# Splitting the recurrence's gate weights: four pieces on ScalarE and VectorE instead of two on GpSimd

## The chip, the cores and the metric

One NeuronCore of a Trainium2 chip runs the whole program. The metric is device time in microseconds (us) for one execution; lower is better. Five engines work side by side, each through its own queue in order: TensorE (PE: matmuls and transposes), VectorE (DVE), ScalarE (ACT), GpSimd (POOL) and SyncE (SP, which issues most DMAs). They wait for one another through semaphores.

## The reference, cut to what matters

A two-layer encoder on 256 tokens of width 1024. Each layer is a SwiGLU block, a mixing step whose two head groups run side by side (a gated linear recurrence, RG-LRU, and windowed attention), and another SwiGLU block:

```python
for l in range(DEPTH):                       # DEPTH = 2
    x = x + 0.5 * swiglu(rms_norm(x, ffn1_norm[l]), ffn1_w_gate[l], ffn1_w_up[l], ffn1_w_down[l])
    h = rms_norm(x, mix_norm[l])
    xr, gate, q, k, v = jnp.split(h @ w_in[l], SPLITS, axis=-1)
    y = concat([rms_norm(recurrent_group(xr, gate, ..., w_a, w_x, ...)), rms_norm(windowed_gqa(q, k, v, ...))])
    x = x + y @ w_out[l]
    x = x + 0.5 * swiglu(rms_norm(x, ffn2_norm[l]), ffn2_w_gate[l], ffn2_w_up[l], ffn2_w_down[l])
return rms_norm(x, final_norm)

# in recurrent_group, for each of two directions d: gates from small block-diagonal weights
r = sigmoid(einsum('bsnc,ncd->bsnd', xb, w_a[d]) + b_a[d])    # 8 blocks of 64 x 64
i = sigmoid(einsum('bsnc,ncd->bsnd', xb, w_x[d]) + b_x[d])
```

## The kernel before, in words

Inputs and outputs are float32. For TensorE every weight `w` is split into a rounded part `wh` (of type fp32r) and the rest, `wl = w - wh`, activations likewise, and a product is the sum of three: high by high, high by low, low by high. The splitting is a stream of its own. SP loads raw weights in pieces of 1 MB into three buffers (`raw`). From each, ACT makes `wh` (L297, 128x1024) and DVE makes `wl` (L298, 128x1024) into a ring of eight slots; a raw buffer is loaded again when both of its halves are split, and a slot is filled again when TensorE has used it.

Six stages follow one another: for each layer a SwiGLU stage (`ffn`), a mixing stage (`mix`) and a second `ffn`. The two `ffn` stages that open a layer are the places of this change; I call them the opening stages of layer 0 and of layer 1. In an `ffn`, the hidden units come in 22 blocks `m` of 128. The first two are done token-major in the head (`natural`, L544, for the first `ffn` `first_head`, L701), gated by ACT (tanh, L724) and DVE (L725, L726), and transposed on TensorE into one PSUM bank (`head_end`, L718), which ACT and DVE split into `hh` and `hl` (L732, L733). From m = 2 on, `gu` runs the gate and the up projection of a block (16 or so matmuls each, L563 to L566) into PSUM, `whole` adds the halves (`sg` and `su`: ACT L744, DVE L745), `gated` and `split_h` make `hh` and `hl` for the down projection, `dn` (L573 to L575). PSUM has two banks under the name `ps_g` and two under `ps_c`, which these projections and the transposes take in turn: a projection has to wait until ACT and DVE have emptied the bank that it gets.

The orders of PE, SP and POOL are as the program is written. Those of ACT and DVE are set by the scheduler that builds the program, by its own estimate of when an instruction becomes ready. Each queue is then worked off in that order.

The gate weights of the recurrence, `gw` (two kinds a, two directions d, four tiles of 128x128: 128x2048 in all), are loaded by POOL in each opening stage: at m == `GLOAD` (4), `load_gates` clears the tile (L355) and issues four DMAs for each a (L359, eight in all per stage). Since POOL has nothing else to do, it does so as soon as its queue comes there. At m == `GSPLIT` (8), `split_gates` lets POOL make `gh_t` (a rounding copy, L369, 128x1024 for each a) and `gl_t` (a subtraction with two SBUF operands, L370, 128x1024 for each a). They are used a stage later, by `lru_gate` in the mixing stage (L887 to L889).

Of the kernel before, what the change touches and what calls it, by code (L numbers as in the profile page):

```python
# [8 lines left out]
F32 = mybir.dt.float32  # L9
F32R = mybir.dt.float32r  # L10
AF = mybir.ActivationFunctionType
ALU = mybir.AluOpType
# [20 lines left out]
TAIL = 4  # L33
HB = 7
GLOAD = 4
GSPLIT = 8
X1 = False
EXTRA = {("kv", 0): "w", ("kv", 1): "i"}
if X1:
# [28 lines left out]
def encoder_kernel(  # L68
# [31 lines left out]
    pe, act, dve, pool = nc.tensor, nc.scalar, nc.vector, nc.gpsimd  # L100
# [250 lines left out]
    gw = []  # L351

    def load_gates(l):
        gw.append(mix_p.tile([128, 2, 2, NT, 128], F32, tag="i", name="gw"))
        pool.memset(gw[l], 0.0)  # L355
        for a, w in ((0, lru_w_a), (1, lru_w_x)):
            for d in range(2):
                for e in range(2):
                    pool.dma_start(  # L359
                        out=gw[l][64 * e:64 * e + 64, a, d, :, 64 * e:64 * e + 64],  # L360
                        in_=w[l, d].rearrange("(t e) c o -> e c t o", e=2)[e],
                    )

    gh_t = const.tile([128, 2, 2, NT, 128], F32R, name="gh_t")
    gl_t = const.tile([128, 2, 2, NT, 128], F32R, name="gl_t")

    def split_gates(l):
        for a in range(2):
            pool.tensor_copy(out=gh_t[:, a], in_=gw[l][:, a])  # L369
            pool.tensor_tensor(out=gl_t[:, a], in0=gw[l][:, a], in1=gh_t[:, a].bitcast(F32), op=ALU.subtract)  # L370

    def load_x(t):
        for hf in range(2):
# [54 lines left out]
    def setup_params():  # L428
        tmp = a_p.tile([128, 2, 512], F32, tag="a", name="tmp")
        rows_t = tmp[:N_ROWS, 0, :]  # L430
        srcs = [(R_CONVW, conv_w.rearrange("l j c -> (l j) c")), (R_CONVB, conv_b),
                (R_BA, lru_b_a.rearrange("l d c -> (l d) c")), (R_BX, lru_b_x.rearrange("l d c -> (l d) c")),
                (R_LAM, lru_lambda.rearrange("l d c -> (l d) c")), (R_GREC, lru_out_norm), (R_GATT, attn_out_norm)]
        for r, s in srcs:
            pool.dma_start(out=rows_t[r:r + s.shape[0], :], in_=s)
        pool.dma_start(out=sink_t, in_=attn_sink.partition_broadcast(128))
        rb = mix_p.tile([128, T], F32, tag="k", name="rb")[:33, :NH]
        oh = tmp[:33, 1, :]
        pool.memset(rb[32:33, :], -1e30)
        pool.dma_start(out=rb[0:32, :], in_=rel_bias)  # L440
        pool.dma_start(out=oh, in_=onehot)
        return tmp, rows_t, rb, oh
# [231 lines left out]
    def ffn(st, acc_done):  # L674
# [38 lines left out]
        def head_end():  # L713
            ps = bank("gc")
            for t in range(2):
                for m in range(2):
                    c = m * T + t * 128
                    pe.transpose(ps[:, c:c + 128], hn_t[t][:, m * 128:(m + 1) * 128], eye_t)  # L718
            for m in range(2):
                split_h(m, ps[:, m * T:(m + 1) * T])  # L720

        def gated(g, u):
            th = ep_p.tile([128, T], F32, tag="th", name="th")
            act.activation(out=th, in_=g, func=AF.Tanh, scale=0.5)  # L724
            dve.scalar_tensor_tensor(out=th, in0=th, scalar=1.0, in1=g, op0=ALU.add, op1=ALU.mult)  # L725
            late["gated"] = dve.tensor_tensor(out=th, in0=th, in1=u, op=ALU.mult)  # L726
            return th

        def split_h(m, src):
            hh = h_p.tile([128, T], F32R, tag="hh", name="hh")  # L730
            hl = h_p.tile([128, T], F32R, tag="hl", name="hl")
            act.activation(out=hh, in_=src, func=AF.Copy)  # L732
            dve.tensor_sub(out=hl, in0=src, in1=hh.bitcast(F32))  # L733
            hh_t[m] = (hh, hl)

        def gu(m, nm):
            ps = gu_ps[m, nm] = bank("gc")
            proj_pair(ps, W(st, nm, m))
            done((st, nm, m))

        def whole(m, nm):
            ps = gu_ps.pop((m, nm))
            s = sum_p.tile([128, T], F32, tag="s" + nm, name="s" + nm)
            act.activation(out=s, in_=ps[:, T:2 * T], func=AF.Copy)  # L744
            dve.tensor_tensor(out=s, in0=ps[:, 0:T], in1=s, op=ALU.add)  # L745
            return s

        def dn(m, t, hfs, fin):
            if t not in acc:
                acc[t] = [bank("ab"[t]) for _ in range(2)]  # L750
            hh, hl = hh_t[m]
            for hf in hfs:
                end = NM - TAIL if st == (DEPTH - 1, 2) and (t, hf) == (1, 1) else NM
                stream(acc[t], hh, hl, W(st, "d", m), t, (hf,), m == 0, m == end - 1)
            if fin:
                done((st, "d", m))
                del hh_t[m]
# [24 lines left out]
        def body():  # L782
            nd = 0
            for m in range(HEAD, NM):
                if m >= RAMP:
                    state["ahead"] = min(DAHEAD, state["ahead"] + 1)
                gu(m, "g")
                g = whole(m, "g")
                gu(m, "u")
                split_h(m, gated(g, whole(m, "u")))  # L790
                if m == HEAD:
                    head_end()
                if st == (0, 0):
                    if m == 4:
                        late_setup.append(setup_params())
                    if m == 9:
                        setup_params2(*late_setup.pop())
                if st[1] == 0 and m == GLOAD:
                    load_gates(st[0])
                if st[1] == 0 and m == GSPLIT:  # L800
                    split_gates(st[0])
                while nd <= m - LAG and nd < NM - TAIL and m > HEAD:
                    dn(nd, 0, (0, 1), False)
                    dn(nd, 1, (0, 1), True)
                    nd += 1
            while nd < NM - TAIL:
                dn(nd, 0, (0, 1), False)
                dn(nd, 1, (0, 1), True)
                nd += 1

        if st == (DEPTH - 1, 2):
            tail, evac = dn_cols, acc
        return head if st != (0, 0) else first_head, body, tail, evac

    def mix(l):
# [378 lines left out]
```

## Time and profile before

| what | value |
|---|---|
| time, median of 3 runs | 952.01 us (951.38 to 953.37) |
| the profiled execution | 952.4 us, of which the traced span is 950.6 us |
| PE busy | 927.3 us, 98% of the span |
| DVE busy | 705.0 us, 74% |
| ACT busy | 540.0 us, 57% |
| POOL busy | 56.4 us, 6% |

The span runs from the first to the last instruction; 1.8 us of the profiled execution lie outside it. Engine names are as above; L12 is line 12 of the kernel before. Times in the trace are us from the span's start. A PE matmul's record overlaps the next one's, so the pace is read from the starts.

### The profile page before, as it was taken

What the parts mean: (1) busy time and instruction counts of PE and PEld (TensorE: products, weight loads), DVE (VectorE), ACT (ScalarE), POOL (GpSimd) and SP (SyncE); (2) the same over time, 40 slices, a digit from 0 to 9 for tenths busy, and PEclk for the clock granted to TensorE, in tenths of its full rate; (3) what the DMA queues carried; (4) which work ended last, traced back from release to release, by engine and by line L of the source; (5) the groups of instructions that cost most, each with busy time, mean ns of one, the idle gap of its engine ahead of it and who ended that gap; (6) DMA issues with size and microseconds to landing.
All of it is one profiled execution on the core that took longest, in us unless ns stands there. A gap on an engine that the chain in (4) does not pass through costs nothing.

```text
span 950.6 us, 13902 instructions
## 1 busy us (share of the span) xinstructions
PE 927.3 (98%) x5407; PEld 811.6 (85%) x5407; DVE 705.0 (74%) x1192; ACT 540.0 (57%) x986; POOL 56.4 (6%) x66
## 2 busy tenths in 40 slices
PE   6799999999999999999999999999999999999997
PEld 6688888889989888888887888888999898888885
DVE  6967766768998866666589666666799887666663
ACT  7555555647864655555455555555587565555542
POOL 4400000000010000000070000000000100000000
PEclk9899999999999999999999999999999999999998
DMA  8865865625254856555646565556152566566521
GB/s 280 261 212 188 301 208 196 204 85 177 90 155 143 278 183 207 186 180 192 204 131 224 180 207 190 179 189 208 45 193 95 180 201 220 180 197 199 178 89 44
DMA packets 124994, 172.56 MB, mean 182 GB/s; under 512 B 3920, under 2 KB 108792, under 8 KB 124928
## 3 DMA queue, kind: packets, MB, share of 16 engines
q1 hardware_dynamic: 122192, 166.21, 54.3%
q0 software_dynamic: 2288, 4.87, 1.6%
q8 instruction: 42, 0.69, 0.3%
q10 hardware_dynamic: 448, 0.59, 0.2%
q14 instruction: 24, 0.20, 0.1%
HBM read 170.59 MB, written 3.16 MB: 183 GB/s over the span
## 4 chain that ended last, share of the span: by engine, by line
PE 91%; DVE 4%; ACT 2%; DMA 2%; issue 1%; POOL 0%; SPq 0%; POOLq 0%; DVEq 0%; ACTq 0%
PE ps_g L564 15%; PE ps_c L564 15%; PE ps_g L563 7%; PE ps_c L563 7%; PE ps_a L573 4%; PE ps_a L575 4%; PE ps_a L574 4%; PE ps_b L575 4%; PE ps_b L574 4%; PE ps_b L573 4%; PE ps_c L544 2%; PE ps_g L544 2%; DVE wl L298 1%; PE ps_a L997 1%; PE ps_g L552 1%
## 5 line engine op out<-in xcount | busy, mean ns | idle before, releaser
L298 DVE TENSOR_TENSOR wl<-raw,wh 128x1024 fp32r<-128x1024 f32 (+1 forms) x308 | 374.3, 1221 | 106.1 <-ACT wh L297 101.1
L297 ACT ACTIVATE wh<-raw 128x1024 fp32r<-128x1024 f32 (+1 forms) x294 | 300.3, 1032 | 87.3 <-PE ps_b L575 63.4
L564 PE MATMUL ps_g<-xhl,wh 128*128 128x512 f32 x640 | 233.7, 399 | 4.9 <-DVE hl L733 4.9
L564 PE MATMUL ps_c<-xhl,wh 128*128 128x512 f32 x640 | 232.6, 398 | 0.0
L563 PE MATMUL ps_g<-xhl,wl 128*128 128x256 f32 x560 | 157.3, 281 | 0.0
L563 PE MATMUL ps_c<-xhl,wl 128*128 128x256 f32 x560 | 156.7, 280 | 0.0
L564 PEld LDWEIGHTS ps_g<-xhl,wh 128*128 128x128 f32 x640 | 121.2, 189 | 28.5 <-issue 5.2
L564 PEld LDWEIGHTS ps_c<-xhl,wh 128*128 128x128 f32 x640 | 121.0, 189 | 23.1
L563 PEld LDWEIGHTS ps_g<-xhl,wl 128*128 128x128 f32 x560 | 106.6, 190 | 3.5
L563 PEld LDWEIGHTS ps_c<-xhl,wl 128*128 128x128 f32 x560 | 106.3, 190 | 3.5
L573 PE MATMUL ps_a<-wh,hh 128*128 128x512 f32 x168 | 65.8, 391 | 0.0
L573 PE MATMUL ps_b<-wh,hh 128*128 128x512 f32 x168 | 65.6, 391 | 0.0
L575 PE MATMUL ps_b<-wh,hl 128*128 128x512 f32 x168 | 65.4, 389 | 0.0
L575 PE MATMUL ps_a<-wh,hl 128*128 128x512 f32 x168 | 65.4, 389 | 0.0
L574 PE MATMUL ps_b<-wl,hh 128*128 128x512 f32 x168 | 65.4, 389 | 0.0
L574 PE MATMUL ps_a<-wl,hh 128*128 128x512 f32 x168 | 65.4, 389 | 0.0
L744 ACT ACTIVATE sg<-ps_g 128x256 f32<-128x256 f32 x40 | 15.4, 384 | 60.5 <-PE ps_g L564 60.2
L744 ACT ACTIVATE sg<-ps_c 128x256 f32<-128x256 f32 x40 | 15.4, 384 | 58.5 <-PE ps_c L564 58.4
L492 POOL TENSOR_TENSOR rstd<-rstd,half_t 128x1 f32<-128x1 f32 x16 | 11.2, 701 | 616.7 <-DVE rstd L489 488.2
L745 DVE TENSOR_TENSOR sg<-ps_g,sg 128x256 f32<-128x256 f32 x40 | 17.0, 425 | 31.8 <-ACT sg L744 31.8
L744 ACT ACTIVATE su<-ps_c 128x256 f32<-128x256 f32 x40 | 15.5, 386 | 40.8 <-PE ps_c L564 40.8
L744 ACT ACTIVATE su<-ps_g 128x256 f32<-128x256 f32 x40 | 15.4, 385 | 40.4 <-PE ps_g L564 40.4
(316 smaller groups left out, 1685.1 us busy)
## 6 DMA issues: line engine op xcount, KB each, us to landing
raw<-in_ffn_w_down_dram SPq DMA_DIRECT2D x44, 1024.0 KB, 5.0
raw<-in_ffn_w_gate_dram SPq DMA_DIRECT2D x43, 1024.0 KB, 5.4
raw<-in_ffn_w_up_dram SPq DMA_DIRECT2D x43, 1024.0 KB, 5.4
raw<-in_w_in_dram SPq DMA_DIRECT2D x14, 1024.0 KB, 5.4
raw<-in_w_out_dram SPq DMA_DIRECT2D x8, 1024.0 KB, 7.5
lb<-ld POOLq DMA_DIRECT2D x1, 2048.0 KB, 14.9
bias_t<-lb POOLq DMA_DIRECT2D x1, 1536.0 KB, 12.2
gain<-in_ffn_norm_dram SPq DMA_DIRECT2D x3, 512.0 KB, 4.4
```

The costliest lines, as they stand in the source:

```text
L297: act.activation(out=h3, in_=src, func=AF.Copy)
L298: dve.tensor_sub(out=l3, in0=src, in1=h3.bitcast(F32))
L492: pool.tensor_tensor(out=st[:, 1:2], in0=st[:, 0:1], in1=half_t, op=ALU.pow)
L544: pe.matmul(dst, (xh, xh, xl)[p][:, k, ts_], w[k // 4][p % 2][:, c], start=(p == 0 and k == 0), stop=(p == 2 and k == KD - 1))
L552: pe.matmul(dst, wh[:, ks], xh[:, k, t0:t1], start=(k == 0), stop=False)
L563: pe.matmul(dst[:, 0:T], wl[:, ks], x2[:, 0, k, :], start=False, stop=False)
L564: pe.matmul(dst, wh[:, ks], x2[:, :, k, :], start=(k == 0), stop=(k == KD - 1))
L573: pe.matmul(acc[hf], ah[:, ts_], wh[:, cs], start=first, stop=False)
L574: pe.matmul(acc[hf], ah[:, ts_], wl[:, cs], start=False, stop=False)
L575: pe.matmul(acc[hf], al[:, ts_], wh[:, cs], start=False, stop=last)
L744: act.activation(out=s, in_=ps[:, T:2 * T], func=AF.Copy)
L745: dve.tensor_tensor(out=s, in0=ps[:, 0:T], in1=s, op=ALU.add)
```

## The change

`split_gates` is called in four steps, at m = 12, 13, 14 and 15, each for one pair (a, d): ACT makes a 128x512 piece of `gh_t` and DVE subtracts a 128x512 piece for `gl_t`. POOL keeps the clearing and the loads, and loses the four splitting instructions of each layer. The changed kernel has one line less from there on, so its L368 and L369 are the new pieces, and each later line has a number one lower (its L723 to L744 are L724 to L745 of before).

```diff
-GSPLIT = 8
+GSPLIT = 12
...
-    def split_gates(l):
-        for a in range(2):
-            pool.tensor_copy(out=gh_t[:, a], in_=gw[l][:, a])
-            pool.tensor_tensor(out=gl_t[:, a], in0=gw[l][:, a], in1=gh_t[:, a].bitcast(F32), op=ALU.subtract)
+    def split_gates(l, a, d):
+        act.activation(out=gh_t[:, a, d], in_=gw[l][:, a, d], func=AF.Copy)
+        dve.tensor_sub(out=gl_t[:, a, d], in0=gw[l][:, a, d], in1=gh_t[:, a, d].bitcast(F32))
...
-                if st[1] == 0 and m == GSPLIT:
-                    split_gates(st[0])
+                if st[1] == 0 and GSPLIT <= m < GSPLIT + 4:
+                    split_gates(st[0], *divmod(m - GSPLIT, 2))
```

The scheduler puts the pieces much earlier than m = 12. The orders of PE and SP stay the same, word for word. In layer 1, ACT's queue at the end of the head reads like this before (`L724 th<-ps_g` is the tanh for the head's second half of the tokens; the `wh` rows split weights):

```order
L297 ACTIVATE wh<-raw 128x1024 x5
L724 ACTIVATE th<-ps_g 128x256
L297 ACTIVATE wh<-raw 128x1024
L744 ACTIVATE sg<-ps_g 128x256
L297 ACTIVATE wh<-raw 128x1024
```

and in the changed kernel:

```order
L297 ACTIVATE wh<-raw 128x1024 x3
L368 ACTIVATE gh_t<-gw 128x512 x3
L297 ACTIVATE wh<-raw 128x1024
L723 ACTIVATE th<-ps_g 128x256
L297 ACTIVATE wh<-raw 128x1024
L368 ACTIVATE gh_t<-gw 128x512
L297 ACTIVATE wh<-raw 128x1024
L743 ACTIVATE sg<-ps_g 128x256
```

Three pieces of `gh_t` stand ahead of the tanh, and one of the five `wh` has moved behind it. DVE's queue at the same place, with the gating of the head (`th`) and the low parts (`wl`), before:

```order
L298 TENSOR_TENSOR wl<-raw,wh 128x1024 x5
L725 SCALAR_TENSOR_TENSOR th<-th,ps_g 128x256
L726 TENSOR_TENSOR th<-th,ps_c 128x256
L298 TENSOR_TENSOR wl<-raw,wh 128x1024
L745 TENSOR_TENSOR sg<-ps_g,sg 128x256
```

and in the changed kernel:

```order
L298 TENSOR_TENSOR wl<-raw,wh 128x1024 x3
L369 TENSOR_TENSOR gl_t<-gw,gh_t 128x512 x2
L724 SCALAR_TENSOR_TENSOR th<-th,ps_g 128x256
L298 TENSOR_TENSOR wl<-raw,wh 128x1024
L725 TENSOR_TENSOR th<-th,ps_c 128x256
L298 TENSOR_TENSOR wl<-raw,wh 128x1024
```

Two pieces of `gl_t` stand ahead of the gating, two `wl` have moved behind its first step, and one of these stands between its two steps. In layer 0 the pieces stand later, in the block after the transposed head has been split. DVE's queue there, in the changed kernel (the L369 rows are new):

```order
L298 TENSOR_TENSOR wl<-raw,wh 128x1024
L725 TENSOR_TENSOR th<-th,su 128x256
L369 TENSOR_TENSOR gl_t<-gw,gh_t 128x512
L744 TENSOR_TENSOR sg<-ps_c,sg 128x256
L369 TENSOR_TENSOR gl_t<-gw,gh_t 128x512
L732 TENSOR_TENSOR hl<-th,hh 128x256
L724 SCALAR_TENSOR_TENSOR th<-th,sg 128x256
L298 TENSOR_TENSOR wl<-raw,wh 128x1024
L744 TENSOR_TENSOR su<-ps_g,su 128x256
L298 TENSOR_TENSOR wl<-raw,wh 128x1024
L725 TENSOR_TENSOR th<-th,su 128x256
L369 TENSOR_TENSOR gl_t<-gw,gh_t 128x512 x2
```

Up to the first of them DVE's order in layer 0 is that of before, and so is ACT's up to its first piece of `gh_t`, which stands at the same place.

## Rows read from the trace of the kernel before

**Rows 1.** The chain that ended last, by engine, from the page.

```profile
PE 91%; DVE 4%; ACT 2%; DMA 2%; issue 1%; POOL 0%; SPq 0%; POOLq 0%; DVEq 0%; ACTq 0%
```

**Rows 2.** TensorE's waits: line, what released it, us in total, times, longest.

```profile
PE ps_g L564 <- DVE hl L733: 4.9, 1, 4.9
...
PE ps_g L718 <- DVE th L725: 2.5, 1, 2.5
...
PE ps_b L527 <- DVE xn L509: 0.9, 2, 0.4
```

**Rows 3.** Timeline of PE, layer 0: start, us, operation, idle before and its releaser.

```profile
42.81 0.76 PE L564 MATMUL ps_g<-xhl,wh 128*128 128x512 f32 x1 [4.93 <-DVE hl L733]
...
48.01 0.40 PE L564 MATMUL ps_c<-xhl,wh 128*128 128x512 f32 x1
```

**Rows 4.** Timeline of PE, layer 0 earlier: transposes, then two projections' first matmuls.

```profile
28.90 0.60 PE L718 MATMUL ps_g<-eye_t,th 128*128 128x128 f32 x4
29.26 0.47 PE L564 MATMUL ps_c<-xhl,wh 128*128 128x512 f32 x1
...
32.12 0.39 PE L564 MATMUL ps_g<-xhl,wh 128*128 128x512 f32 x1
```

**Rows 5.** Busy time by stretch: PE, PEld, DVE, ACT, POOL, granted clock, DMA share, GB/s.

```profile
43.00:47.80 4.80, 4.80 (x16) 4.12 (x17) 4.80 (x8) 2.58 (x5) 0.00 (x0) 0.50 0.75 230
...
489.40:499.20 9.80, 8.71 (x58) 7.72 (x57) 9.80 (x5) 5.66 (x8) 9.59 (x5) 1.00 0.87 279
...
502.00:505.20 3.20, 3.20 (x12) 2.71 (x11) 3.17 (x7) 1.71 (x4) 0.00 (x0) 0.50 0.97 310
```

**Rows 6.** Timeline of POOL, layer 0: the second subtraction.

```profile
35.55 3.23 POOL L370 TENSOR_TENSOR gl_t<-gw,gh_t 128x1024 fp32r<-128x1024 f32 x1
```

**Rows 7.** Timeline of DVE, layer 0, beside POOL's splitting and behind it.

```profile
29.94 2.06 DVE L298 TENSOR_TENSOR wl<-raw,wh 128x1024 fp32r<-128x1024 f32 x1 [0.43 <-ACT wh L297]
31.93 0.41 DVE L745 TENSOR_TENSOR su<-ps_c,su 128x256 f32<-128x256 f32 x1
32.26 2.29 DVE L725 SCALAR_TENSOR_TENSOR th<-th,sg 128x256 f32<-128x256 f32 x1
...
36.47 2.59 DVE L726 TENSOR_TENSOR th<-th,su 128x256 f32<-128x256 f32 x1
...
40.45 0.41 DVE L733 TENSOR_TENSOR hl<-ps_g,hh 128x256 fp32r<-128x256 f32 x1
```

**Rows 8.** DVE's split of 128x1024 from 100 to 200 us: count, busy us, mean ns.

```profile
L298 DVE TENSOR_TENSOR wl<-raw,wh 128x1024 fp32r<-128x1024 f32 x33 | 40.4, 1225 | 15.9 <-ACT wh L297 15.2
```

**Rows 9.** Timeline of ACT, layer 0, while POOL splits.

```profile
33.72 2.02 ACT L297 ACTIVATE wh<-raw 128x1024 fp32r<-128x1024 f32 x2 [2.28 <-DMA raw<-in_ffn_w_down_dram]
...
35.63 0.37 ACT L744 ACTIVATE sg<-ps_c 128x256 f32<-128x256 f32 x1
```

**Rows 10.** Timeline of PE, layer 1: the transposes, and the projection of block 3's up half.

```profile
500.62 0.97 PE L718 MATMUL ps_g<-eye_t,th 128*128 128x128 f32 x4 [2.51 <-DVE th L725]
...
505.78 0.39 PE L564 MATMUL ps_g<-xhl,wh 128*128 128x512 f32 x1
```

**Rows 11.** Timeline of DVE, layer 1, from the head's end.

```profile
488.26 11.98 DVE L298 TENSOR_TENSOR wl<-raw,wh 128x1024 fp32r<-128x1024 f32 x5
```

**Rows 12.** Timeline of ACT, layer 1, from the head's end.

```profile
487.14 2.98 ACT L297 ACTIVATE wh<-raw 128x1024 fp32r<-128x1024 f32 x3
...
491.48 2.01 ACT L297 ACTIVATE wh<-raw 128x1024 fp32r<-128x1024 f32 x2 [1.36 <-PE ps_g L544]
```

**Rows 13.** Splits of the size of the new pieces, from the program's start: ns min/median/max.

```profile
L258 ACT ACTIVATE wh<-raw x8: 630/646/680, 6.2 to 16.6; 128x512 fp32r<-128x512 f32 x8
```

**Rows 14.** The same on DVE.

```profile
L256 DVE TENSOR_TENSOR wl<-raw,wh x8: 680/684/686, 8.1 to 18.3; 128x512 fp32r<-128x512 f32 x8
```

**Rows 15.** The loads of the gate weights, layer 1: POOL's issues, and their landing.

```profile
L359 POOL DMA_DIRECT2D gw<-in_lru_w_x_dram x4: 629/640/649, 487.0 to 488.8; - x4
...
DMA to landing us min/median/max: 2.2/2.4/3.2
```

## The prediction, made before the changed kernel was run

> **What bounds the kernel now.** I read the chain of work that ended last first. TensorE is 91% of it [rows 1], so a microsecond counts only where TensorE stands still or runs slowly. TensorE's own waits come next. Outside the program's start the view has only three kinds: one of 4.9 us for `hl` (L733), one of 2.5 us for `th` (L725), and two of at most 0.4 us [rows 2]. The first lies in layer 0's opening stage at 37.88 to 42.81 [rows 3], the second in layer 1's at 498.11 to 500.62 [rows 10]. Both are waits for DVE, and both lie where POOL splits the gate weights. So I looked at DVE there.
>
> In layer 0 three of DVE's instructions are drawn out while POOL works [rows 7]: a split of 128x1024 took 2.06 us, against 1.225 us as a mean of 33 elsewhere [rows 8]; the two steps of the gating took 2.29 and 2.59 us, against the 0.41 us of other 128x256 steps. POOL's second subtraction ran from 35.55 to 38.78 [rows 6]; DVE's step beside it began at 36.47 and ended at 39.06, 0.28 us after POOL. It looks as if DVE's step could not run until POOL's was over. A step with one operand in PSUM, `su`, took its normal 0.41 us at 31.93. In layer 1, five splits took 11.98 us [rows 11], or 2.4 us each in place of 1.2, nearly all of it in a stretch of 9.8 us in which POOL was busy for 9.59 [rows 5]. That is the cost of POOL's four instructions per layer: not the time that they take on POOL, but what they do to DVE.
>
> A second loss follows each wait. The granted clock was 0.50 from 43.0 to 47.8 and from 502.0 to 505.2 [rows 5], the lower of TensorE's two levels, 1.2 in place of 2.4 GHz. The projection that began at 42.81 took until 48.01, 5.20 us [rows 3]; one at full clock took 32.12 - 29.26 = 2.86 us [rows 4].
>
> **The change, part by part.** *POOL's splitting goes.* Its own time costs nothing. What it gives back I follow through DVE's queue.
>
> Layer 0. DVE's split at 29.94 would end at 31.16 (1.22 us), `su` at 31.6, the first gating step at 32.0, the next split at 33.2 and the second gating step at 33.6, against 39.06 now. DVE is then not the last any more. The next split needs `wh`, and ACT starts it only at 33.72, when its raw weights have landed [rows 9]; POOL had no part in that. The pair of `wh` took 2.02 us, `sg` started at 35.63, and `hh<-th` behind it would run from 35.9 to 36.3. Meanwhile DVE's split (34.7 to 36.0) is over, so `hl<-th` starts at about 36.35 and the first `hl<-ps_g` at 36.7. In the trace it started at 40.45 [rows 7], and TensorE 2.36 us later; between them DVE and ACT do the same work in the same order as before. So TensorE goes on at about 39.1. It gains 42.81 - 39.1 = 3.7 us and still waits 1.2 us. If the clock stays up for that, the projection takes 2.86 and not 5.20 us, 2.3 us more. Bounds for this layer: 3.7 (the clock falls all the same) and 7.2 (no wait is left). I take 6.0, since the remaining wait rests on the row of a DMA that the change doesn't touch.
>
> Layer 1. TensorE was ready at 500.62 - 2.51 = 498.11 and began block 3's up projection at 505.78 [rows 10], 7.67 us later. Without a wait and at full clock the same transposes and projection took 32.12 - 28.90 = 3.22 us [rows 4]. The most to be had is 4.45 us. It is had if DVE has done both gating steps by 498.11, with the new pieces in the way.
>
> *ACT's and DVE's new pieces.* One costs 0.65 us on ACT [rows 13] and 0.68 us on DVE [rows 14]: 2.6 and 2.7 us a layer, in place of some 6 us by which DVE was drawn out. In layer 0 they stand behind the instruction that releases TensorE, where in the trace DVE catches up anyhow: the next TensorE wait for DVE is in a later stage and 0.4 us long at most [rows 2]. I cost them at nothing there; if that cover were gone, at most 2.7 us.
>
> In layer 1 they stand ahead. ACT's three `wh` end at 490.12 [rows 12], three pieces of `gh_t` at 492.1, one `wh` at 493.1, and the tanh at 493.5. In the trace ACT waited 1.36 us before the fourth `wh` [rows 12], so part of this fills a hole. DVE: three splits at 1.22 from 488.26 end at 491.9, two pieces of `gl_t` at 493.3, the first gating step, waiting for the tanh, at 493.9, a split at 495.2, the second step at 495.6. TensorE needs them at 498.11; 2.5 us are to spare. The next need is the split of the transposed head, for block 4's up projection: TensorE is there at 498.11 + 0.36 + 3 x 2.86 = 507.1. DVE begins its list for it when ACT has emptied `su`, at about 498.6: eight steps of 0.41, two or three splits and one piece of `gl_t`, some 7 us, done by 505.8. Nothing is late, by 1.3 us.
>
> *The wait of ACT for the loads.* Where POOL waited for the gate weights before, ACT does now, and the tanh is queued behind it. POOL issues the third pair of loads from 486.98, at 0.64 us each, and a load lands 2.2 to 3.2 us after its issue [rows 15]: by 491.5 at the latest, while ACT comes to the third piece at about 491.4. I cost it at nothing; the cover is the 2.5 us above.
>
> The sum: 3.7 + 2.3 + 4.45 = 10.5 us. TensorE's order is unchanged and it waits for nothing of weight later on [rows 2], so the gain should reach the end. The profiled execution took 952.4 us, which gives 941.9. The median of the runs is 0.4 us lower, so I predict 941.5.
>
> **The rivals.** *The clock falls in layer 0 in spite of the shorter wait* (18%). It fell after waits of 4.93 and 2.51 us; no row shows one of 1.2 us, and the 0.4 us waits are too short to tell. The price is what the two rows show beside the wait: 2.3 us in layer 0, 7.67 - 3.22 - 2.51 = 1.9 us in layer 1. That gives 943.4 to 943.8.
>
> *A new wait takes part of the gain in layer 1* (8%). The margins of 2.5 and 1.3 us rest on summed durations. If ACT comes late through the loads, or DVE through its list, TensorE pays each us beyond the margin, and a wait of over 2 us may bring the clock down again: 942 to 946.
>
> *DVE was drawn out by something else, and gets heavier* (4%). The DMA share beside it was 0.87 [rows 5], so heavy loading could be the cause. Then the splits stay at 2.4 us, the pieces cost 1.4 us each in proportion, and two of them stand ahead of the gating in layer 1: three splits, two pieces, then a split between the steps give 488.26 + 7.2 + 2.8 + 0.4 + 2.4 + 0.4 = 501.5 for the second step, which ended at 501.1 before. Behind it come 1.4 us more ahead of the split of the transposed head. Slower by 0.4 to 2 us: 952.5 to 954. It decides against the change only if a two-operand step stays drawn out without POOL. The normal `su` in the middle of it, and the end 0.28 us after POOL's end, speak against it.
>
> The Trainium skill, Perfetto Trace Analysis, section Optimizing Scalar/DVE Operations, bears on this rival: where DVE is saturated, moving work to ScalarE or even GpSimd may make sense, though the two share a read port, so that it might not help. DVE was busy for all of that stretch, so by the first half of that sentence the change goes the wrong way; by the second half it does not. The trace agrees with the second: the work that was kept off DVE cost it more (some 6 us in layer 1) than it would have itself (2.7 us).
>
> **How the numbers follow.** My forecast has 70%, the rivals 18, 8 and 4%. The range runs from 939.8 (no wait left in layer 0, and 0.5 us for the spread of runs) to 945.5, which takes in the clock's rival and most of the new wait. A measurement can tell about 0.2%, 1.9 us, from no change: faster 96%, same 3%, slower 1%.
>
> **What would show it.** POOL without its four instructions at each place; DVE's splits at 1.2 us throughout; TensorE's waits down to one of about 1.2 us for `hl` in layer 0 and none for `th` in layer 1; a granted clock of 1.00 in both stretches. A DVE step over 2 us there, a wait of ACT before `gh_t`, or a projection of 5 us behind the remaining wait would each prove a step wrong.

## The result, and the profile after

The changed kernel took 941.86 us (median of 4 runs, 941.66 to 943.2) against 952.27 us for the kernel before (951.38 to 953.37): a ratio of 0.9895, interval 0.9883 to 0.9907, or 10.4 us less. Predicted were 941.5 us, between 939.8 and 945.5.

The profiled execution of after was the slowest of the four: 943.2 us, of which the span is 941.4. The first lines come from its page: the busy time of each engine, and the chain of work that ended last, by engine.

```profile
PE 923.3 (98%) x5407; PEld 808.5 (86%) x5407; DVE 696.3 (74%) x1200; ACT 543.7 (58%) x994; POOL 38.0 (4%) x58
...
PE 92%; DVE 3%; DMA 2%; ACT 2%; issue 1%; POOL 0%; ACTq 0%; POOLq 0%; DVEq 0%; SPq 0%
```

VectorE has been given work and yet is busy for 8.7 us less than before (705.0 us). TensorE is busy for 4.0 us less (927.3 before), with the same matmuls. The chain is still TensorE's, as in [rows 1]. The view of TensorE's waits (line and releaser, us in total, times, longest) shows the rest; line numbers from L368 on are one lower than before:

```profile
PE ps_b L389 <- DMA eye_t<-in_eye_dram: 5.4, 1, 5.4
PE ps_a L415 <- DVE xn L405: 2.3, 1, 2.3
PE ps_g L551 <- DVE xc L866: 1.0, 1, 1.0
PE ps_g L563 <- DVE hl L732: 1.0, 1, 1.0
PE ps_b L526 <- DVE xn L508: 0.9, 2, 0.4
```

Against [rows 2]: the wait for `hl` went from 4.9 to 1.0 us, the one for `th` is gone. The first two lines are the program's start, which before had as well. A wait of 1.0 us in the mixing stage (L551) is new; I come to it below.

Layer 0. TensorE's timeline (start, us, idle before and its releaser), which answers to [rows 3]:

```profile
39.36 0.47 PE L563 MATMUL ps_g<-xhl,wh 128*128 128x512 f32 x1 [0.95 <-DVE hl L732]
...
42.25 0.40 PE L563 MATMUL ps_c<-xhl,wh 128*128 128x512 f32 x1
```

The projection behind the wait took 42.25 - 39.36 = 2.89 us, where it had taken 5.20. DVE's timeline at the same place, for [rows 7]:

```profile
30.55 1.22 DVE L298 TENSOR_TENSOR wl<-raw,wh 128x1024 fp32r<-128x1024 f32 x1 [0.48 <-ACT wh L297]
...
32.10 0.41 DVE L724 SCALAR_TENSOR_TENSOR th<-th,sg 128x256 f32<-128x256 f32 x1
...
33.57 0.42 DVE L725 TENSOR_TENSOR th<-th,su 128x256 f32<-128x256 f32 x1
35.14 1.22 DVE L298 TENSOR_TENSOR wl<-raw,wh 128x1024 fp32r<-128x1024 f32 x1 [1.15 <-ACT wh L297]
...
37.00 0.42 DVE L732 TENSOR_TENSOR hl<-ps_g,hh 128x256 fp32r<-128x256 f32 x1
```

The same steps that took 2.06, 2.29 and 2.59 us take 1.22, 0.41 and 0.42. DVE now waits 1.15 us for ACT, and ACT's row says for what, as in [rows 9]: the raw weights of the down projection.

```profile
34.04 2.01 ACT L297 ACTIVATE wh<-raw 128x1024 fp32r<-128x1024 f32 x2 [2.01 <-DMA raw<-in_ffn_w_down_dram]
```

Layer 1. First DVE, then ACT, then TensorE, for [rows 10 to 12]:

```profile
483.67 3.50 DVE L298 TENSOR_TENSOR wl<-raw,wh 128x1024 fp32r<-128x1024 f32 x3
487.08 1.28 DVE L369 TENSOR_TENSOR gl_t<-gw,gh_t 128x512 fp32r<-128x512 f32 x2
488.34 0.42 DVE L724 SCALAR_TENSOR_TENSOR th<-th,ps_g 128x256 f32<-128x256 f32 x1
...
489.81 0.41 DVE L725 TENSOR_TENSOR th<-th,ps_c 128x256 f32<-128x256 f32 x1
...
500.49 0.42 DVE L732 TENSOR_TENSOR hl<-ps_g,hh 128x256 fp32r<-128x256 f32 x1
```

```profile
485.40 1.69 ACT L368 ACTIVATE gh_t<-gw 128x512 fp32r<-128x512 f32 x3
...
487.91 0.40 ACT L723 ACTIVATE th<-ps_g 128x256 f32<-128x256 f32 x1
```

```profile
493.36 0.60 PE L717 MATMUL ps_g<-eye_t,th 128*128 128x128 f32 x4
...
496.62 0.40 PE L563 MATMUL ps_g<-xhl,wh 128*128 128x512 f32 x1
...
502.22 0.40 PE L563 MATMUL ps_g<-xhl,wh 128*128 128x512 f32 x1
```

DVE's gating was over at 490.22, 3.1 us before TensorE came for it. Transposes and projection took 496.62 - 493.36 = 3.26 us, where they had taken 7.67. The windows of before [rows 5] and two like them in after (columns as there; the clock is the last but two):

```profile
39.00:47.80 8.80, 8.44 (x48) 7.43 (x49) 8.80 (x16) 7.46 (x14) 0.00 (x0) 1.00 0.88 292
489.40:499.20 9.80, 9.80 (x60) 8.55 (x59) 9.29 (x15) 7.32 (x13) 0.00 (x0) 1.00 1.05 368
```

The granted clock is 1.00 in both, and POOL is idle. Last, the new pieces themselves (ns min/median/max, first and last start), eight on ACT and eight on DVE:

```profile
L368 ACT ACTIVATE gh_t<-gw x8: 614/633/651, 44.2 to 489.1; 128x512 fp32r<-128x512 f32 x8
...
L369 DVE TENSOR_TENSOR gl_t<-gw,gh_t x8: 680/684/684, 46.4 to 503.3; 128x512 fp32r<-128x512 f32 x8
```

### The profile page after: what moved, and what is told of

It reads as the page before. It is cut to its first block, busy times and chain, and to the rows that moved or that the text cites. A ratio compares the mean times of both kernels' runs of the same rounds, so it can differ in the third digit from the quotient of the medians.

```text
span 941.4 us, 13900 instructions
## 1 busy us (share of the span) xinstructions
PE 923.3 (98%) x5407; PEld 808.5 (86%) x5407; DVE 696.3 (74%) x1200; ACT 543.7 (58%) x994; POOL 38.0 (4%) x58
## 4 chain that ended last, share of the span: by engine, by line
PE 92%; DVE 3%; DMA 2%; ACT 2%; issue 1%; POOL 0%; ACTq 0%; POOLq 0%; DVEq 0%; SPq 0%
PE ps_g L563 15%; PE ps_c L563 15%; PE ps_g L562 7%; PE ps_c L562 7%; PE ps_a L572 5%; PE ps_a L574 4%; PE ps_a L573 4%; PE ps_b L574 4%; PE ps_b L572 4%; PE ps_b L573 4%; PE ps_c L543 2%; PE ps_g L543 2%; PE ps_a L996 1%; PE ps_g L551 1%; PE ps_g L552 1%; PE ps_g L553 1%
## 5 line engine op out<-in xcount | busy, mean ns | idle before, releaser
L298 DVE TENSOR_TENSOR wl<-raw,wh 128x1024 fp32r<-128x1024 f32 (+1 forms) x308 | 366.3, 1195 | 107.0 <-ACT wh L297 102.3
L744 DVE TENSOR_TENSOR sg<-ps_g,sg 128x256 f32<-128x256 f32 x40 | 17.0, 425 | 32.4 <-ACT sg L743 32.4
L573 PEld LDWEIGHTS ps_a<-wl,hh 128*128 128x128 f32 x168 | 31.6, 188 | 6.9
L574 PEld LDWEIGHTS ps_a<-wh,hl 128*128 128x128 f32 x168 | 31.5, 188 | 6.9
```

The source lines that it names most:

```text
L298: dve.tensor_sub(out=l3, in0=src, in1=h3.bitcast(F32))
L573: pe.matmul(acc[hf], ah[:, ts_], wl[:, cs], start=False, stop=False)
L574: pe.matmul(acc[hf], al[:, ts_], wh[:, cs], start=False, stop=last)
```

## The experiments

Two questions were open: whether POOL's splitting is the cause of DVE's long steps, and by what (its presence, its writes, its reads, its place), and what sets the microsecond that TensorE still waits in layer 0. Diffs are against the changed kernel unless said otherwise. Each time stands beside runs of the kernel before on the same chip.

### No splitting at all

```diff
-    def split_gates(l, a, d):
-        act.activation(out=gh_t[:, a, d], in_=gw[l][:, a, d], func=AF.Copy)
-        dve.tensor_sub(out=gl_t[:, a, d], in0=gw[l][:, a, d], in1=gh_t[:, a, d].bitcast(F32))
+    for w in (gh_t, gl_t):
+        pool.memset(w.bitcast(F32), 0.0)
...
-                if st[1] == 0 and GSPLIT <= m < GSPLIT + 4:
-                    split_gates(st[0], *divmod(m - GSPLIT, 2))
```

> No splitting of the gate weights at all: GpSimd clears both tiles once at the program's start, and neither ScalarE nor VectorE gets the pieces (the gates are then computed from zeros; that work is left out). Theory (GpSimd's splitting held VectorE up, and the new pieces lie in slack): the time of the changed kernel, 941.9 us, within 0.6. Rival (the pieces cost something where they stand, up to 2.7 us a layer): faster than the changed kernel by up to 5.4 us, 936.5. If GpSimd's work was not the cause, 952.

942.39 us (941.76 to 944.28), ratio 0.9907 [0.9892, 0.9922]: the time of the changed kernel. The pieces cost nothing that can be measured. The profiled run, the slowest of its four, shows the first rival by chance: the down projection's weights came later, TensorE waited 2.12 us, and the clock fell. Timelines of ACT and TensorE, then a window:

```profile
34.86 2.01 ACT L297 ACTIVATE wh<-raw 128x1024 fp32r<-128x1024 f32 x2 [2.91 <-DMA raw<-in_ffn_w_down_dram]
```

```profile
40.18 0.47 PE L563 MATMUL ps_g<-xhl,wh 128*128 128x512 f32 x1 [2.12 <-DVE hl L732]
```

```profile
42.00:45.00 3.00, 3.00 (x11) 2.52 (x10) 3.00 (x6) 2.20 (x5) 0.00 (x0) 0.50 0.78 294
```

### One layer each

In the first kernel POOL splits in layer 0 as before and ACT and DVE split in layer 1; the second is the reverse (`st[0] == 1` for POOL).

```diff
+    def split_pool(l):
+        for a in range(2):
+            pool.tensor_copy(out=gh_t[:, a], in_=gw[l][:, a])
+            pool.tensor_tensor(out=gl_t[:, a], in0=gw[l][:, a], in1=gh_t[:, a].bitcast(F32), op=ALU.subtract)
...
-                if st[1] == 0 and GSPLIT <= m < GSPLIT + 4:
+                if st[1] == 0 and st[0] == 0 and m == 8:
+                    split_pool(0)
+                if st[1] == 0 and st[0] == 1 and GSPLIT <= m < GSPLIT + 4:
```

> The change in layer 1 alone: in layer 0 GpSimd splits as before. Theory: layer 1's share of the gain, 4.5 us, so 947.8, with VectorE drawn out and TensorE waiting 4.9 us in layer 0 only. Rival (one cause common to both places, as a lower clock that follows from the first wait): the gain is nearly all or nothing, 942 or 952.

> The change in layer 0 alone: in layer 1 GpSimd splits as before. Theory: layer 0's share, 6.3 us in the two traces, so 946.0, with TensorE waiting 2.5 us in layer 1 only. Rival: as for the run with GpSimd in layer 0, 942 or 952.

Layer 1 alone: 947.55 us (947.42 to 948.4), 4.1 less than before's 951.61 on that chip. Layer 0 alone: 945.65 us (945.43 to 946.97), 6.0 less. The forecast's terms were 4.45 and 6.0. Together they make 10.1, so the two layers add up. The wait that is left in each (TensorE's waits, first and second kernel) is that of before:

```profile
PE ps_g L568 <- DVE hl L737: 4.8, 1, 4.8
```

```profile
PE ps_g L722 <- DVE th L729: 2.5, 1, 2.5
```

### POOL busy, but only writing

```diff
-                if st[1] == 0 and GSPLIT <= m < GSPLIT + 4:
-                    split_gates(st[0], *divmod(m - GSPLIT, 2))
+                if st[1] == 0 and m == 8:
+                    for _ in range(3):
+                        for w in (gh_t, gl_t):
+                            pool.memset(w.bitcast(F32), 0.0)
```

> No splitting (left out), but in its place GpSimd clears the two tiles three times each, six writes of 1.8 us, about 11 us in all in each layer and at the same place in its queue: it writes SBUF for as long as before, and reads nothing. Theory A (VectorE's two-operand steps are held up by a GpSimd instruction that reads SBUF): VectorE's splits stay at 1.2 us, 941.9. Theory B (any GpSimd instruction on SBUF holds them up): splits of 2 us or more, and a time near 952.

942.32 us (941.63 to 942.89), ratio 0.9903 [0.9888, 0.9917]. In layer 0 POOL was busy from 26.52 to 37.10 with six clears like the one shown, and DVE beside it kept its pace: three splits in 3.70 us, gating steps of 0.41 us. DVE's timeline, layer 0 and layer 1, then POOL's:

```profile
27.09 3.70 DVE L298 TENSOR_TENSOR wl<-raw,wh 128x1024 fp32r<-128x1024 f32 x3
...
31.11 0.41 DVE L721 SCALAR_TENSOR_TENSOR th<-th,sg 128x256 f32<-128x256 f32 x1
...
483.32 3.50 DVE L298 TENSOR_TENSOR wl<-raw,wh 128x1024 fp32r<-128x1024 f32 x3
```

```profile
30.03 1.83 POOL L799 MEMSET gh_t<- 128x2048 f32 x1
```

So it isn't that POOL runs, nor that it writes to SBUF. What the clears leave out of the splitting is that it reads (and calculates with what it has read).

This trace answers a rival too: that in layer 1 the scheduler's new order ended the wait for `th`, since in the changed kernel two of the five splits stand behind the gating's first step. Here all five stand ahead of the gating, as in the kernel before (and as in the kernels with no splitting and with POOL's splitting held back). The gating was over at 490.85 all the same, and TensorE didn't wait for it.

### POOL's splitting, held back to the middle of the stage

This is the kernel before, with POOL's splitting behind a small copy that reads the activations of block 12, so that it can't run earlier:

```diff
-GSPLIT = 8
+GSPLIT = 12
...
+                    pool.tensor_copy(out=tick, in_=hh_t[m][0][:, 0:1].bitcast(F32))
                     split_gates(st[0])
```

> GpSimd splits as before, whole, but later: a one-column copy that reads block 12's hidden units stands ahead of it in GpSimd's queue, so it falls in the middle of both opening stages, where VectorE is ahead of TensorE. Theory A (the stretch of VectorE costs only where TensorE is about to wait for it): VectorE's steps beside it are drawn out as before, some 6 us a layer, but TensorE waits little, and the time is within 2 us of the changed kernel's 941.9. Theory B (the stretch itself costs, wherever it is): 950 to 952.

943.44 us (942.97 to 943.89), ratio 0.991 [0.9895, 0.9925]: with POOL still splitting, 8.5 of the 10.4 us are there. POOL now works at 109 to 118 us in layer 0 and at 571 to 581 us in layer 1, and DVE is drawn out there and nowhere else. DVE, POOL, and the window, in layer 0:

```profile
114.95 1.25 DVE L727 SCALAR_TENSOR_TENSOR th<-th,sg 128x256 f32<-128x256 f32 x1
116.13 0.41 DVE L747 TENSOR_TENSOR su<-ps_g,su 128x256 f32<-128x256 f32 x1
116.57 2.20 DVE L728 TENSOR_TENSOR th<-th,su 128x256 f32<-128x256 f32 x1
```

```profile
113.90 2.02 POOL L371 CAST gh_t<-gw 128x1024 fp32r<-128x1024 f32 x1
116.00 2.49 POOL L372 TENSOR_TENSOR gl_t<-gw,gh_t 128x1024 fp32r<-128x1024 f32 x1
```

```profile
108.40:118.50 10.10, 10.10 (x55) 8.62 (x55) 7.68 (x8) 4.04 (x6) 9.90 (x5) 1.00 0.84 281
```

Each drawn-out gating step ended 0.28 us after the POOL instruction beside it (116.20 after 115.92, 118.77 after 118.49), the very distance of [rows 6, 7]. `su`, with an operand in PSUM, ran in the middle of POOL's subtraction in its normal 0.41 us. A drawn-out split of 128x1024 ended 1.07 to 1.09 us after POOL's instruction, here and in the kernel before, which is nearly the 1.22 us that it takes alone: DVE's step isn't slower beside POOL, it starts late. POOL is held as well: its copy at 113.90 took 2.02 us beside the end of such a split, where two copies of the next kernel, with DVE idle when they began, took 1.05 us each.

DVE's steps are drawn out by 2.9 us a layer here, not by the 6 us expected. DVE was busy for 7.68 of 10.10 us and TensorE for all of them: here DVE's delay is free. So the loss takes both, POOL's reading and a place where TensorE waits for DVE.

The rest to the changed kernel, some 1.5 us, is lost elsewhere, as far as the trace shows. At the end of layer 0's opening stage TensorE waited 0.8 and 0.7 us (for `xn` and `xhl`), and the scheduler had moved a split of the next stage's weights to 196.8 us, between the steps that these waits need; in the changed kernel it ran at 177.9. That it is the cause is read from the order of the rows and wasn't tried alone.

### POOL rounds, DVE subtracts

In this kernel POOL makes `gh_t`, at block 12:

```diff
-        act.activation(out=gh_t[:, a, d], in_=gw[l][:, a, d], func=AF.Copy)
+        if d == 0:
+            pool.tensor_copy(out=gh_t[:, a], in_=gw[l][:, a])
```

> The change by half: GpSimd keeps the rounding copy (two of 1.1 us in each layer, one SBUF operand), VectorE gets the four subtractions. Theory: a copy holds a VectorE step up by 0.9 us; in layer 0 that is two copies, 1.7 us, against the 1.1 us by which VectorE waited for ScalarE in the changed kernel, in layer 1 several us are to spare: 941.9 to 943. Rival (GpSimd's long two-operand subtractions are not what matters, its presence is): 947 to 952.

947.96 us (946.4 to 950.71, 7 runs), ratio 0.9962 [0.995, 0.9973]: 6 us worse than expected. DVE's timeline at the end of layer 0's opening stage and the entry in TensorE's waits say why:

```profile
197.19 2.49 DVE L370 TENSOR_TENSOR gl_t<-gw,gh_t 128x512 fp32r<-128x512 f32 x4
199.60 1.27 DVE L509 SCALAR_TENSOR_TENSOR xn<-x,rstd,gain 128x256 f32<-128x256 f32 x3
```

```profile
PE ps_a L527 <- DVE xn L509: 2.8, 2, 1.6
```

The scheduler put all four pieces of `gl_t` at the border between two stages, ahead of the norm for which TensorE waits there. A split of the next stage's weights (1.22 us at 200.86) stands between the norm's steps as well, as in the kernel of the section before, which lost some 1.5 us there. The granted clock was 0.50 behind the waits, from 201.5 to 208.3. So some 4.5 of the 6 us are left for pieces of normal length (0.62 us each) in the wrong place and the low clock behind them; that share is an estimate from the two kernels and wasn't tried alone. The same pieces where the changed kernel has them cost nothing.

The same division of work at block 8 (POOL's copies moved to m == 8, DVE's four pieces where they were):

```diff
-        act.activation(out=gh_t[:, a, d], in_=gw[l][:, a, d], func=AF.Copy)
...
+                if st[1] == 0 and m == 8:
+                    for a in range(2):
+                        pool.tensor_copy(out=gh_t[:, a], in_=gw[st[0]][:, a])
```

> The half change again, with GpSimd's two rounding copies ahead of its setup loads, so that they run at about 30 us and 489 us as in the kernel before, and VectorE's subtractions stand away from the end of the stage. Theory: a copy of 1.1 us holds one VectorE step up by at most 0.9 us; in layer 0 up to 1.7 us of that meets 1.1 us of slack, in layer 1 several us are to spare: 941.9 to 943, and no subtraction ahead of the norm at the end of layer 0's opening stage. Rival (GpSimd's presence costs, as the 948.0 of the first half change would say): 947 or more.

941.94 us (941.62 to 944.7), ratio 0.9899 [0.9884, 0.9915], as the changed kernel. DVE's timeline, layer 0 and layer 1, beside POOL's first copy, which ran from 29.70 to 31.59:

```profile
31.00 0.85 DVE L723 SCALAR_TENSOR_TENSOR th<-th,sg 128x256 f32<-128x256 f32 x1
...
482.19 5.28 DVE L298 TENSOR_TENSOR wl<-raw,wh 128x1024 fp32r<-128x1024 f32 x3
```

A copy, which reads one operand, holds DVE too: the gating step ended at 31.85, again 0.26 us after POOL, and three splits in layer 1 took 5.28 us against 3.50 in the changed kernel. That is less than the margin in layer 1, so TensorE doesn't see it.

### Two pieces for four

```diff
+    def split_gates(l, a):
+        act.activation(out=gh_t[:, a], in_=gw[l][:, a], func=AF.Copy)
+        dve.tensor_sub(out=gl_t[:, a], in0=gw[l][:, a], in1=gh_t[:, a].bitcast(F32))
...
+                if st[1] == 0 and GSPLIT <= m < GSPLIT + 2:
+                    split_gates(st[0], m - GSPLIT)
```

> The changed kernel with two pieces of 128x1024 in place of four of 128x512, on the same engines. Theory (the pieces lie in slack of over 1 us): no difference, 941.9 within 0.6. Rival (a long piece in ScalarE's or VectorE's queue holds up the gating): slower by up to 1.2 us a layer, 943 to 944.

941.78 us (941.07 to 942.37), ratio 0.9891 [0.9876, 0.9906]. The size of the pieces doesn't matter.

### The wait that is left

TensorE's wait for `hl` in layer 0 differs between kernels that do the same there. In each of them TensorE goes on 5.3 us after ACT could start on the down projection's weights:

| kernel | ACT starts at, us | TensorE goes on at, us | TensorE has waited, us |
|---|---|---|---|
| no splitting | 34.86 | 40.18 | 2.1 |
| POOL rounds at block 12 | 34.43 | 39.74 | 1.0 |
| the changed kernel, second run (below) | 34.36 | 39.68 | 2.0 |
| the changed kernel | 34.04 | 39.36 | 0.95 |
| change in layer 0 alone | 33.94 | 39.25 | 1.3 |
| POOL writes | 33.82 | 39.14 | 1.3 |
| two pieces | 33.58 | 38.89 | 1.1 |
| POOL rounds at block 8 | 33.55 | 38.86 | 1.2 |
| POOL's splitting held back | 32.85 | 38.17 | 0.05 |

The wait doesn't follow ACT's start alone, because TensorE comes there at 37.6 to 38.7 us, depending on when the program's first load landed (4.6 to 5.5 us). In the kernel before ACT started at 33.72 [rows 9]; 5.3 us more give 39.0, where the prediction had 39.1. The gate loads that POOL issues from 21.7 us on, and an SP load of a gain of 512 KB, run beside these weights. Holding both back to block 6 in layer 0 tests whether they are in the way (the small copy into `tick` reads block 6, so that POOL has to wait for it):

```diff
+                if st == (0, 0) and m == 6:
+                    load_gain(1)
+                    pool.tensor_copy(out=tick, in_=hh_t[m][0][:, 0:1].bitcast(F32))
-                if st[1] == 0 and m == GLOAD:
+                if st[1] == 0 and m == (GLOAD, 6)[st == (0, 0)]:
...
-        load_gain(1)
```

> The changed kernel, with the loads of the gate weights and of the next gain in layer 0 held back to block 6, when the start's burst of weight loads is over. Theory (what is left of layer 0's wait, 0.95 us, is ScalarE waiting for the raw weights to land, which share the DMA engines with these loads): the weights land over 1 us earlier, the wait goes, 941.0. Rival (the wait has another cause behind it, or the weights land no sooner): 941.9.

The changed kernel ran once more beside it, on the same chip:

> The changed kernel once more. If the wait of 1.0 us for the convolution in layer 0's mixing stage was one load that landed late in the profiled run, it is absent or in another place, and the time is 941.9; if the change brings it, it is there again at the same matmul.

940.37 us (939.95 to 940.49) with the loads later, 942.89 (941.76 to 944.31) without. ACT began on the weights at 30.89, not at 34.36, and TensorE's wait is gone; beside it, it was 2.0 us long. The second run of the changed kernel was expected at 941.9 and is 1 us slower.

Which of the two loads was it? First the gain alone:

```diff
+                if st == (0, 0) and m == 6:
+                    load_gain(1)
...
-        load_gain(1)
```

> The changed kernel with only the load of the next gain (0.5 MB) held back to block 6 in layer 0; the gate weights are loaded as before. Theory: the raw weights of the down projection land about 1 us earlier, since the gain is issued just behind them, and the weights of the up projection, ahead of it, do not: half to all of the gain of the run with both loads later, 940.4 to 941.5. Rival (the gate weights' loads on GpSimd's queue are what delays the raw weights): 941.9.

942.76 us (941.51 to 942.92), ratio 0.9897 [0.9881, 0.9914]: not what was expected. ACT's timeline:

```profile
29.20 0.63 ACT L368 ACTIVATE gh_t<-gw 128x512 fp32r<-128x512 f32 x1 [2.76 <-DMA gw<-in_lru_w_a_dram]
...
34.12 2.01 ACT L297 ACTIVATE wh<-raw 128x1024 fp32r<-128x1024 f32 x2 [0.50 <-DMA raw<-in_ffn_w_down_dram]
```

The weights were as late as ever. From issue to landing (last column, us; loads between 19 and 35 us) they took

```profile
raw<-in_ffn_w_down_dram SPq DMA_DIRECT2D x1, 1024.0 KB, 7.8
```

no less than with the gain beside them (7.6 us in the changed kernel, 8.7 in its second run). So the gain alone isn't what delays them. TensorE waited 2.2 us, though without a fall of the clock (last column but two of the window):

```profile
38.00:49.00 11.00, 8.84 (x50) 7.77 (x51) 10.37 (x17) 8.23 (x16) 0.00 (x0) 1.00 0.80 250
```

The scheduler had also put pieces of `gh_t` earlier: ACT waited 2.76 us for the gate loads, with the splitting of weights queued behind, and TensorE went on 6.0 us after ACT's start on the down projection's weights, not 5.3. So the length of this wait doesn't compare with the others. The gate loads alone do better:

```diff
+                if st == (0, 0) and m == 6:
+                    pool.tensor_copy(out=tick, in_=hh_t[m][0][:, 0:1].bitcast(F32))
-                if st[1] == 0 and m == GLOAD:
+                if st[1] == 0 and m == (GLOAD, 6)[st == (0, 0)]:
```

> The changed kernel with only the loads of the gate weights (0.5 MB in eight DMAs on GpSimd's queue) held back to block 6 in layer 0; the gain is loaded as before. With the gain alone moved the down projection's raw weights landed no sooner and the time did not fall, so the theory is now that the gate weights' loads delay them: landing at 31 to 32 us, a wait of TensorE for the split head of under 0.3 us, 940.4 to 941. Rival (only both together leave the DMA engines enough room): 941.5 to 942.5, with a wait of 1 to 2 us.

939.93 us (939.77 to 940.87), ratio 0.9874 [0.9857, 0.989], the fastest of all. TensorE's waits, and the start of ACT on the weights:

```profile
PE ps_b L391 <- DMA eye_t<-in_eye_dram: 4.6, 1, 4.6
PE ps_a L417 <- DVE xn L407: 2.3, 1, 2.3
PE ps_b L528 <- DVE xn L510: 0.9, 2, 0.4
```

```profile
30.87 2.01 ACT L297 ACTIVATE wh<-raw 128x1024 fp32r<-128x1024 f32 x2 [0.98 <-DMA raw<-in_ffn_w_down_dram]
```

From issue to landing the down projection's weights took 7.6 us in the changed kernel and 5.2 here (5.0 where the gain was held back too):

```profile
raw<-in_ffn_w_down_dram SPq DMA_DIRECT2D x1, 1024.0 KB, 7.6
```

```profile
raw<-in_ffn_w_down_dram SPq DMA_DIRECT2D x1, 1024.0 KB, 5.2
```

So the gate loads, eight of 64 KB, delay the weights, and taking them away is enough to end the wait. Not all of the 3.4 us between the two spans (941.4 and 938.0) is theirs. By the starts of the same matmuls, 0.8 us comes from the program's start, 1.1 from the wait for `hl`, 1.2 from the mixing stage, and 0.3 from small steps behind that.

## Why the prediction was right

Starts of the same matmul in both profiled executions (TensorE's order is the same) give each step its measured size. All of after stands 0.54 us late from the start, since the load that TensorE waits for first came at 5.4 us.

- **Layer 0: 6.0 predicted, 6.3 measured.** The end of the wait moved from 42.81 to 39.36, 4.0 us without that 0.54 (3.7 predicted); the projection behind it went from 5.20 to 2.89 us, 2.3 us, as predicted. The wait left was put at 1.2 us and was 0.95; with the weights 0.32 us later and TensorE 0.53 us later than in the kernel before, that agrees. The reason held: ACT waits for a DMA. DVE's second gating step ended at 33.99 (33.6 predicted, 39.06 before). The prediction counts three DVE steps drawn out; there were four, since the split at 34.48 took 2.07 us too. Its path reckons that one at its normal length, so nothing hangs on it.
- **Layer 1: 4.45 predicted, 7.67 - 3.26 = 4.4 measured.** The margins held as well. The gating had 3.1 us to spare (2.5 predicted). The split of the transposed head ended at 500.91, and TensorE came to block 4's up projection at 502.22: 1.3 us, as predicted, but by luck, since DVE began its list 0.6 us later than reckoned and took 6.4 us for it, not 7. ACT didn't wait for the gate loads.
- **The new pieces: nothing predicted, nothing measured.** Their lengths were those of [rows 13, 14], and the kernel without any splitting is no faster. But the run with `gl_t` at the border of two stages shows that this rests on the place.
- **The sum: 10.5 predicted; 10.4 between the medians (9.1 in the second series, 942.89 against 951.96), 9.2 in the profiled execution.** The steps make 6.3 + 4.4 = 10.7. The profiled execution then lost 0.54 at the start and 1.1 in layer 0's mixing stage. The other three runs of after took 941.66 to 941.92.
- **The gain reaches the end: not quite in every run.** The wait in the mixing stage has no part in the sum. DVE's timeline there:

```profile
214.54 0.69 DVE L295 CAST wh<-raw 128x1024 fp32r<-128x1024 f32 x1 [1.43 <-DMA raw<-in_w_in_dram]
```

DVE's queue stood for 1.43 us until a load landed, and the convolution (`xc`) that TensorE needs stood behind. The kernel with layer 0 left as before has the same wait of 1.0 us, and the one in which POOL only writes has 0.8 us; the ones with no splitting and with two pieces don't have it, and the changed kernel's second run has it in layer 1's mixing stage. It comes and goes with a late load, not with the change. Why that load is late in some runs stays open.

The rivals. *The clock* does fall at times: it fell in the run without splitting, after 2.1 us, and that run took some 2 us longer than the others of its kernel. The low clock itself cost 1.5 us of that (by the starts of the same matmuls beside the run with two pieces), less than the 2.3 us it was priced at. It didn't after 0.95, 1.3 and, in the changed kernel's second run, 2.0 us; nor after the 2.2 us of the run that moved the gain's load. So at about 2 us it goes either way, and the wait's length alone doesn't tell which; what does stays open. The chance of 18% was given to a wait of 1.2 us, after which it fell in no profiled run; but the wait is as long as the weights are late in a given run. Of the changed kernel's eight runs one, of 944.31 us, shows a lower mean clock (0.996, against 0.998 or 0.999); it has no trace, so where the clock fell in it isn't known. *A new wait in layer 1* didn't come. *Something else that draws DVE out* is refuted: with a DMA share of 1.05 DVE's steps are normal in after, and with POOL's splitting at 109 and 571 us they are long there and nowhere else. In the traces of the seven kernels in which POOL neither rounds nor subtracts, no split of 128x1024 and no gating step is drawn out at all.

## What to carry to other kernels

Work handed to an idle engine isn't free if the two hold each other up, as POOL and DVE do here when both read SBUF: look at the mean duration of the same instruction beside it and away from it, and let the busy engine do the work itself if that costs it less than it is held. Then ask where the delay is paid. The same splitting on POOL cost 10 us where TensorE was about to wait for DVE; in the middle of a stage TensorE didn't wait beside it. Small loads that nobody needs yet are worth holding back from a stretch in which a large one is waited for.

## What the runs showed of the hardware

- A DVE step with two SBUF operands doesn't slow down beside POOL's reading, it stands: steps of 0.41 us ended 0.26 to 0.28 us after POOL's instruction at four places, splits of 1.22 us 1.07 to 1.09 us after it. It stands beside a subtraction (two operands read) and a copy (one), not beside a clear (none), and a DVE step with an operand in PSUM isn't held at all (0.41 us). POOL stands in its turn when DVE's step was there first: a copy of 1.05 us took up to 2.05 us. The Trainium skill, SBUF — State Buffer, section SBUF: two separate sides, says the same: the port pair that the two share is "an exclusive lock, not a bandwidth split", and a DVE operation with two SBUF inputs meets it only against a GpSimd operation that reads. The trace agrees in each of these points.
- Loads of 0.5 MB in all (eight of 64 KB) on POOL's queue lengthened the landing of 1 MB from 5.2 us to 7.6 us, and to 8.7 us in another run of the same kernel. ACT could begin 3.2 us earlier without them (30.87 against 34.04), 0.8 us of which is the program's start.
- The granted clock stayed at 1.00 (2.4 GHz) behind waits of 0.95 to 2.0 us and behind one of 2.2 us; behind one of 2.1 us it fell to 0.50 (1.2 GHz) for some 3 us.
